# Output projection's second half and first routed expert of a hybrid encoder block: other waits, other queues, another order

## Chip, cores, metric

One core of a Trainium2 chip runs the whole block in one launch. The metric is device microseconds of that core; lower is better. Engines are named as in the profile: PE (TensorE matmul), DVE (VectorE), ACT (ScalarE), POOL (GpSimd), SP (SyncE, which here only issues DMAs).

## What is computed

One encoder layer on 512 tokens of width 1024, all float32. The part that matters here is the last third:

```python
mix = jnp.concatenate([rec, att], axis=-1) @ w_out[l]      # recurrence group | attention group
x = x + g1[:, None, :] * mix
h2 = _rms(x, norm2_g[l]) * (1.0 + sc2[:, None, :]) + sh2[:, None, :]
x = x + g2[:, None, :] * _hier_moe(h2, ...)                # top-1 group of 4, top-2 of its 4 experts
...
# _hier_moe: logits = hf @ w_rg + b_rg, hf @ w_re + b_re; then for each of the 16 experts
he = jax.nn.silu(hf @ w1[e]) * (hf @ w3[e])
y = y + combine[:, e:e + 1] * (he @ w2[e])
```

`g1, sh2, sc2, g2` are slices of `silu(c) @ w_ada + b_ada`. Before this come the adaLN norm, one input projection, a gated linear recurrence (4 heads) and a sparse attention (8 heads).

## The kernel before

Each weight piece (128 x 1024) is split into two fp32r halves, `wh` (a cast on ACT) and `wl` (the rest, a subtraction on DVE), and a product is three matmuls: high by high, low by high, high by low. The program has two parts. Up to line 1304 a planner (`Desk`) runs generators as tasks: each `yield` names an engine, marks that must be set, or a free slot, and the planner picks the next task by a planned time and a rank from `RANKS`. What comes out is a fixed order of instructions on each engine; at run time every engine takes its own list in order, and so does every queue: a DMA that waits holds what stands behind it on the issuing engine. From line 1305 on the order is that of the code.

- `ada_gen` (line 993) computes the vectors g1, sh2, sc2, g2 on DVE: 64 loads `dd` of 256 KB, issued by SP (line 1002), each followed by one DVE accumulation `acc<-dd` with 6 `dd` buffers. Eight loads make a group of 512 columns; then PE sums over partitions (`a<-acc,ones`), ACT copies, and POOL writes the group to `modD` in DRAM (line 1030). `mod_rows` (line 988, on POOL) reads a vector back, spread over all partitions. Groups 0 and 1 are g1, 2 and 3 sh2, 4 and 5 sc2, 6 and 7 g2.
- `rows_gen` (line 1110) starts when all eight groups are done: it reads `gs2b`, `sh2b`, `g2b`, multiplies the norm weights in, transposes both vectors on PE, and folds them into the router's weights `wr` and bias `cb`.
- `out_gen` (line 1148) is the output projection, `z<-wh,mix`. Half 0 takes the recurrence heads; half 1 takes the attention heads and starts when attention, `rows` and `early` (the first eight expert weights' loads) are done. Half 1 runs over 4 tiles of 128 tokens by 2 column halves, 12 matmuls each.
- `post_gen` (line 1199), per token tile: sum of squares, transpose of the residual, router logits, and a chain of small DVE operations that ends in `sel`, the two chosen experts, and `oh0`, a one-hot matrix that puts the tokens of expert 0 into slots. `store_gen` (line 1273) makes the rows `h2`: the scaling on DVE for tiles 0 and 1, on POOL and ACT for 2 and 3, and the addition of `sh2b` on POOL for all four; then ACT issues two stores. `first_gen` (line 1287) gathers expert 0's tokens on PE, `z<-oh,h`, from the finished rows.
- After line 1304: positions and weights of all experts, then `turn(0)` (the gathered tokens, split and transposed), and `up(0, ...)`, the first expert's first product, `h<-wh,xh`, 24 matmuls for `w1` and 24 for `w3`. `piece()` splits four pieces ahead, with four buffers. After the second piece of `w1`, `begin` (line 1520) runs, which makes the index lists of experts 0, 1, 2 (`match`, `place`: `oh<-slotb`, `pI<-pair,oh`) and starts the gathers of 1 and 2. All other experts gather by indirect DMA.

Of the kernel before, what the change touches and what calls it, by code (L numbers as in the profile page):

```python
# [21 lines left out]
KT = D // P  # L22
# [16 lines left out]
RANKS = "split -2 use -2 iq -1 topk 4 unit 1 att 1 hgrn 3 level 4 rows 3 ada 5 load 5 out 6 pz 7 post 0 first 3 norm -3 hx -1"  # L39
# [7 lines left out]
H2_D = 0, 1  # L47
POST_D = 1,
# [166 lines left out]
def hymba_kernel(ctx, tc, x, xT, w_ada1, w_ada, w_in, w_out, w_r, w1, w3, w2, vec, n2g, rb, rel, cst, t5, out):  # L215
# [894 lines left out]
    def rows_gen():  # L1110
        yield ["ada1"]
        mod_rows(gs2b, 4)
        mod_rows(sh2b, 2)
        mod_rows(g2b, 6)
        n2b = place4("A7", [P, D], F32, "n2b")
        sp.dma_start(n2b, bass.AP(tensor=n2g.tensor, offset=n2g.offset, ap=[[0, P], [1, D]]))
        desk.at = desk.move()
# [27 lines left out]

    h2s, routed, px = [None] * 4, {}, []

    def out_gen():
        nonlocal mw, sel, oh0, pair2
        for half in range(2):  # L1150
            if half:
                yield [("att", j) for j in range(4)] + ["rows", "early"]
# [4 lines left out]
                loads(EWB + MWB)  # L1157
# [41 lines left out]
    def post_gen(t):  # L1199
# [7 lines left out]
        for kh in range(2):  # L1207
# [8 lines left out]
            if kh:  # L1216
                mark(("turned", t))
# [14 lines left out]
        spawn(store_gen(t, h2), ("store", t), "post")  # L1232
# [21 lines left out]
        dve.tensor_scalar(oh0[:, t], slotb, p0, float(T), op0=OP.subtract, op1=OP.is_equal)  # L1254
        mark(mb)
# [49 lines left out]
    loads(LOADS1)
    OH, XE = {}, {}
# [23 lines left out]

    pn = bank([P, 4, 16])
    pe.matmul(pn, trib, sel, start=True, stop=False)
    for s in range(1, 4):
        pe.matmul(pn[:, s:], onesb, sel[:, :4 - s], start=False, stop=s == 3)
    pos = mw.tile([P, 4, 16], F32, name="pos")
    dve.scalar_tensor_tensor(pos, pn, 1.0, sel, op0=OP.add, op1=OP.mult)
    dve.tensor_scalar(posb, pos, -1.0, None, op0=OP.add)

    gate, w = (mw.tile([P, 4, n], F32, name=m) for n, m in ((2, "gate"), (1, "wn")))
    ge, comb, rest = (mw.tile([P, 4, n], F32, name=m) for n, m in ((4, "ge"), (16, "comb"), (16, "rest")))  # L1340
    dve.tensor_tensor(ge, L[:, :, 4:8], routed["g1"][:, :, 0:1].to_broadcast([P, 4, 4]), op=OP.subtract)
    dve.tensor_tensor(comb, routed["em"], routed["e2"][:, :, 0:1].to_broadcast([P, 4, 16]), op=OP.subtract)
    act.activation(ge, ge, AF.Exp)
    act.activation(comb, comb, AF.Exp)
    dve.tensor_tensor(comb, comb, sel, op=OP.mult)
    dve.reduce_sum(gate[:, :, 0:1], ge, axis=AX)
# [9 lines left out]
    pc = bank([P, 16])
    for t in range(4):
        pe.matmul(pc, onesb, sel[:, t], start=t == 0, stop=t == 3)
    cmx = mw.tile([P, 1], I32, name="cmx")
    dve.reduce_max(cmx, pc, axis=AX)  # L1360
    mixer.close()


    pq = ctx.enter_context(tc.tile_pool(name="pq", bufs=1, space=PSUM))

    def split2(n):
        if n >= NP or n in split_w:
            return
        raw = held[n]
        own = mw if n % (WPB + WX) >= WPB else wp  # L1370
        wh = own.tile([P, D], F32R, tag="wh", name="wh", bufs=WX if own is mw else WPB)
        wl = own.tile([P, D], F32R, tag="wl", name="wl", bufs=WX if own is mw else WPB)
        act.copy(wh, raw)
        dve.tensor_tensor(wl, raw, wh.bitcast(F32), op=OP.subtract)
        split_w[n] = wh, wl
        load(n + NS)

    count = [0]

    def piece():  # L1380
        n = count[0]
        count[0] += 1
        for i in range(WPB + WX):
            split2(n + i)
        return split_w.pop(n)

    pI = pq.tile([P, 16, 5], F32, tag="i", name="pI")
    XT, HS, HT = {}, {}, {}

    def place(e):  # L1390
        oh = OH.pop(e)
        for t in range(4):
            pe.matmul(pI[:, e], oh[:, t], pair2[:, t, e], start=t == 0, stop=t == 3)
        dve.tensor_scalar(idx[:, e:e + 1], pI[:, e, 0:1], pI[:, e, 1:2], float(T), op0=OP.add, op1=OP.add)
        dve.reduce_sum(wts[:, e:e + 1], pI[:, e, 2:5], axis=AX)
# [16 lines left out]
    def up(e, w, mid=None):  # L1412
# [107 lines left out]
    def begin():  # L1520
        for e in range(3):
            match(e)
            place(e)
            if e:
                gather(e)
                for n in range(*((LOADS1, LOADS2) if e == 1 else (LOADS2, NS))):
                    load(n, pool)

    turn(0)
    for e in range(16):  # L1530
        h1 = up(e, 0, None if e else begin)
# [113 lines left out]
```

## Time and profile before

| | us |
|---|---|
| median of 3 runs (lowest 763.68, highest 1159.99) | 764.67 |
| profiled execution | 764.32 |
| its span, first to last instruction | 762.5 |
| PE busy in the span | 697.0 (91%) |
| DVE busy | 637.9 (84%) |
| ACT busy | 439.8 (58%) |
| POOL busy | 126.4 (17%) |

Busy times are sums over one execution; the shares are averages over stages with different limits, so the stretches of the span are read one by one below. The profiled execution lies 1.8 us above its span and 0.35 us below the median.

### The profile page before, as it was taken

The page shows a single profiled execution, that of the slowest core. Times are in us where ns is not written, and L with a number is a line of the kernel's source. Part 1 is how long each engine was busy: PE and PEld are TensorE (multiplying, and loading weights), DVE is VectorE, ACT ScalarE, POOL GpSimd, SP SyncE. Part 2 cuts the span into 40 slices and gives each one's busy share as a digit, 9 for nine tenths or more (in the row PEclk, how much of TensorE's full clock was granted, in tenths as well). Part 3 has the DMA queues.
Part 4 walks back from the last instruction along what each step waited for, and adds up shares of the span by engine and source line. Part 5 has one row for each costly group of instructions (what it writes and reads, how often), then busy time and mean ns, then how long its engine had stood idle before and what let it go on. Part 6 is the DMA issues. An engine that isn't in the chain of part 4 may idle for free. (4 is left out here: it accounts for less than half of the span.)

```text
span 762.5 us, 10938 instructions
## 1 busy us (share of the span) xinstructions
PE 697.0 (91%) x3790; PEld 539.5 (71%) x3790; DVE 637.9 (84%) x1055; ACT 439.8 (58%) x668; POOL 126.4 (17%) x111
## 2 busy tenths in 40 slices
PE   3999999999999999998179858999999999999993
PEld 1566778877878776765068747888887888888872
DVE  4537989999999888878437577999999999999992
ACT  4326555455586465533032337777777777777870
POOL 0130010013111312210102411111111112111112
PEclk9999999999999999999569978999999999999997
DMA  9946622222221245736874779999999999999202
GB/s 362 394 143 215 221 70 84 93 73 73 80 70 48 106 142 190 272 108 197 316 283 160 266 285 377 320 362 365 364 372 362 371 358 353 359 357 365 88 11 32
DMA packets 57389, 172.85 MB, mean 227 GB/s; under 512 B 11954, under 2 KB 12530, under 8 KB 56304
## 3 DMA queue, kind: packets, MB, share of 16 engines
q1 hardware_dynamic: 45024, 150.02, 53.8%
q0 software_dynamic: 10864, 17.76, 8.3%
q10 hardware_dynamic: 1440, 4.31, 1.5%
q8 instruction: 32, 0.52, 0.3%
q14 instruction: 29, 0.24, 0.1%
HBM read 167.50 MB, written 15.24 MB: 240 GB/s over the span
## 5 line engine op out<-in xcount | busy, mean ns | idle before, releaser
L179 DVE TENSOR_TENSOR wl<-w,wh 128x1024 fp32r<-128x1024 f32 x168 | 196.7, 1217 | 6.2 <-ACT wh L179 5.6
L179 ACT CAST wh<-w 128x1024 fp32r<-128x1024 f32 x168 | 174.0, 1053 | 46.7 <-PE h L179 37.2
L179 PE MATMUL z<-hx,wh 128*128 128x512 f32 x496 | 162.7, 408 | 1.7 <-DVE hx L179 0.8
L179 PEld LDWEIGHTS z<-hx,wh 128*128 128x128 f32 x496 | 88.2, 188 | 28.2 <-issue 8.4
L179 PE MATMUL h<-wh,xh 128*128 128x512 f32 x256 | 103.3, 403 | 4.7 <-ACT wh L179 4.7
L179 ACT CAST wh<-raw 128x1024 fp32r<-128x1024 f32 x64 | 67.1, 1051 | 65.2 <-PE z L179 54.7
L179 PE MATMUL h<-wl,xh 128*128 128x512 f32 x256 | 104.2, 407 | 0.3 <-DVE wl L179 0.3
L179 PE MATMUL h<-wh,xl 128*128 128x512 f32 x256 | 102.8, 402 | 0.0
L179 PE MATMUL z<-hx,wl 128*128 128x512 f32 x248 | 97.5, 393 | 0.0
L179 DVE TENSOR_TENSOR wl<-raw,wh 128x1024 fp32r<-128x1024 f32 x64 | 82.0, 1295 | 6.6 <-ACT wh L179 6.4
L179 PEld LDWEIGHTS h<-wh,xh 128*128 128x128 f32 x256 | 49.5, 193 | 17.5 <-ACT wh L179 4.8
L179 PEld LDWEIGHTS h<-wl,xh 128*128 128x128 f32 x256 | 49.4, 193 | 12.3 <-DVE wl L179 0.8
L179 PEld LDWEIGHTS h<-wh,xl 128*128 128x128 f32 x256 | 49.2, 192 | 11.8
L1318 POOL DMA_INDIRECT out_dram<-yo,idx x16 | 36.0, 2250 | 126.5 <-DVE yo L179 126.5
L179 PE MATMUL y<-wh,hh 128*128 128x512 f32 x128 | 53.4, 417 | 2.0 <-DVE yo L179 2.0
L179 PEld LDWEIGHTS z<-hx,wl 128*128 128x128 f32 x248 | 46.6, 188 | 10.8 <-DVE wl L179 0.7
L179 PE MATMUL y<-wl,hh 128*128 128x512 f32 x128 | 51.3, 401 | 0.0
L179 PE MATMUL y<-wh,hl 128*128 128x512 f32 x128 | 51.2, 400 | 0.0
L179 PE MATMUL z<-wh,mix 128*128 128x512 f32 x128 | 48.1, 428 | 0.0
L179 DVE SCALAR_TENSOR_TENSOR acc<-dd,cT,acc 128x512 f32<-128x512 f32 x56 | 45.4, 810 | 2.5 <-DMA dd<-in_w_ada_dram 1.7
L1313 POOL DMA_INDIRECT xe<-h2D,idx x15 | 16.4, 1090 | 136.6 <-DMA out_dram<-yo,idx 63.7
L179 POOL TENSOR_TENSOR dd<-b 128x512 f32<-128x512 f32 (+1 forms) x14 | 16.5, 1197 | 93.4 <-PE a L179 79.0
(292 smaller groups left out, 1169.8 us busy)
## 6 DMA issues: line engine op xcount, KB each, us to landing
w<-in_w_dram SPq DMA_DIRECT2D x163, 512.0 KB, 11.3
raw<-in_w_in_dram SPq DMA_DIRECT2D x33, 512.0 KB, 3.3
dd<-in_w_ada_dram SPq DMA_DIRECT2D x64, 256.0 KB, 4.0
raw<-in_w_dram SPq DMA_DIRECT2D x24, 512.0 KB, 10.4
chunk<-in_w_ada_dram SPq DMA_DIRECT2D x8, 1024.0 KB, 9.0
raw<-in_w_out_dram SPq DMA_DIRECT2D x8, 512.0 KB, 3.3
lineR<-lineD POOLq DMA_DIRECT2D x4, 640.0 KB, 17.6
w<-in_w_dram POOLq DMA_DIRECT2D x5, 512.0 KB, 8.1
```

The costliest lines, as they stand in the source:

```text
L179: r = f(*a, **k)
L1313: pool.indirect_dma_start(out=dst, out_offset=None, in_=h2D, in_offset=bass.IndirectOffsetOnAxis(ap=ix, axis=0), bounds_check=T - 1, oob_i ...
L1318: pool.indirect_dma_start(out=out, out_offset=bass.IndirectOffsetOnAxis(ap=ix, axis=0), in_=y, in_offset=None, bounds_check=T - 1, oob_is_ ...
```

## The change

The ada loads go from SP's queue to POOL's. `rows_gen` reads `sh2b` and `gs2b` after group 5 instead of after group 7, and `g2b` is read by a task of its own; half 1 no longer waits for `rows`, only for the opening of the memory that the ada groups held. The scaled rows `h2 = xm * gs2b` are made on DVE for all four tiles, the factor `ss2` goes into `oh0`, and `sh2b` comes in through eight matmuls with one row; so expert 0 is gathered before the rows are finished, and these are finished on DVE afterwards. The first four expert pieces are split while half 1 runs. Copies of the transposed residual are all on ACT. After the planner's part, `turn(0)` comes first, and the weights and index lists are spread over `up(0)` and the following product.

```diff
-RANKS = "split -2 ... norm -3 hx -1"
+RANKS = "split -2 ... norm -3 hx -1 store 8 early 9"
-H2_D = 0, 1
-POST_D = 1,
...
-                sp.dma_start(t, w_ada[k * P:(k + 1) * P, 2 * D + g * 512:2 * D + g * 512 + 512])
+                pool.dma_start(t, w_ada[k * P:(k + 1) * P, 2 * D + g * 512:2 * D + g * 512 + 512])
...
-        desk.at += 2500
+            if g == 5:
+                mark("ada_rows")
...
-        yield [("hgrn", 3), "ada0"] + ["ada1"] * DD_R
+        yield [("hgrn", 3), ("split", NZ + 3), "ada0"] + ["ada1"] * DD_R
...
+        mark("early_open")
...
     def rows_gen():
-        yield ["ada1"]
-        mod_rows(gs2b, 4)
-        mod_rows(sh2b, 2)
-        mod_rows(g2b, 6)
         n2b = place4("A7", [P, D], F32, "n2b")
...
+        yield ["ada_rows"]
+        desk.at += 2500
+        mod_rows(gs2b, 4)
+        desk.at = mod_rows(sh2b, 2)
+        yield ["mw"]
...
+    def gate_gen():
+        yield ["ada1"]
+        desk.at += 2500
+        desk.at = mod_rows(g2b, 6)
...
-                yield [("att", j) for j in range(4)] + ["rows", "early"]
+                yield [("att", j) for j in range(4)] + ["early_open"]
...
-            eng, cp_ = (dve, dve.tensor_copy) if kh in POST_D else (act, act.copy)
-            yield eng.name
-            cp_(hT[:, kh * 4:kh * 4 + 4], pt)
+                spawn(scale_gen(t, h2), ("scaled", t), "store")
+            yield "act"
+            act.copy(hT[:, kh * 4:kh * 4 + 4], pt)
             mark(mb)
+            yield ["rows"]
...
+        dve.tensor_scalar(oh0[:, t], oh0[:, t], ss2[:, t:t + 1], None, op0=OP.mult)
...
+    def scale_gen(t, h2):
+        yield ["rows"]
+        yield "dve"
+        dve.tensor_tensor(h2, xm[t], gs2b, op=OP.mult)
...
+    def store(t, h2):
+        dve.scalar_tensor_tensor(h2, h2, ss2[:, t:t + 1], sh2b, op0=OP.mult, op1=OP.add)
         act.dma_start(h2D[t * P:(t + 1) * P, :], h2)
         act.dma_start(out[t * P:(t + 1) * P, :], xm[t])
...
+        for k in range(KT):
+            yield "pe"
+            pe.matmul(px[k // 4][:, k % 4], sh2b[0:1, k * P:(k + 1) * P], ones[0:1], start=False, stop=False)
         for t in range(4):
-            yield [("store", t), ("sel", t)] + [("pr", 3)] * (t > 0)
+            yield [("scaled", t), ("sel", t)]
...
+    def first_weights_gen():
+        yield ["early"]
+        for n, piece in ((0, 4), (3, 5), (1, 6), (2, 7)):
+            yield [("used", NZ + piece)]
+            yield "act"
+            split2_high(n)
+            if n != 2:
+                yield [("sel", 3)] * (n == 1)
+                yield "dve"
+                split2_low(n)
...
+    turn(0)
+    split2_low(2)
+    store(3, h2s[3])
...
         for n in range(4):
-            if n == 2 and mid:
-                mid()
             wh, wl = piece()
+            if e == 0:
+                begin(4 * w + n)
...
+    def begin(n):
+        if n == 0:
+            match(1)
+            place(1, 0, 2)
+            gather(1)
...
+        if n == 2:
+            weigh()
+        if n == 4:
+            match(2)
+            place(2)
+            gather(2)
...
+        if n == 6:
+            match(0)
+            place(0)
+            place(1, 2, 5)
```

On PE, where half 1 begins: `a<-acc,ones` and `a<-cs,vc` are the last ada group's sums, `z<-wh,mix` half 1, and `sh2b`, `gs2b`, `shT` the router vectors. Before:

```order
L179 MATMUL a<-acc,ones 32x128
L179 MATMUL a<-cs,vc 32x128
L179 MATMUL a<-cs,sh2b 128x128 x4
L179 MATMUL a<-cs,gs2b 128x128 x4
L179 MATMUL o<-wr,shT 128x20 x4
L179 MATMUL a<-cs,sh2b 128x128 x4
L179 MATMUL a<-cs,gs2b 128x128 x4
L179 MATMUL o<-wr,shT 128x20 x4
L179 MATMUL z<-wh,mix 128x512
```

And the change, at the same place:

```order
L177 MATMUL a<-acc,ones 32x128
L177 MATMUL a<-cs,vc 32x128
L177 MATMUL z<-wh,mix 128x512
L177 MATMUL z<-wl,mix 128x512
L177 MATMUL z<-wh,mix 128x512 x2
L177 MATMUL z<-wl,mix 128x512
L177 MATMUL z<-wh,mix 128x512
L177 MATMUL a<-cs,sh2b 128x128 x4
```

The vectors' transposes moved from ahead of half 1 into it; the sums of the last ada group still stand ahead of the first `z`.

On POOL, from the write of ada group 5 (the first `modD` here) on, in the change; before, POOL had three `modD` writes and three reads there and no load:

```order
L1028 DMA modD<-acc 4x128
L987 DMA gs2b<-modD 128x1024
L987 DMA sh2b<-modD 128x1024
L1000 DMA dd<-in_w_ada_dram 128x512 x8
L1028 DMA modD<-acc 4x128
L1000 DMA dd<-in_w_ada_dram 128x512 x5
L1028 DMA modD<-acc 4x128
L987 DMA g2b<-modD 128x1024
```

The last thirteen ada loads stand behind two `modD` writes and two reads of `modD` on one queue.

On DVE, from the last tile's `oh0` on. Before, the positions and weights of all experts came first (`pos` to `cmx`), then `xl` of `turn(0)` and the splits:

```order
L179 TENSOR_SCALAR sel<-er 128x16
L179 TENSOR_SCALAR oh_3629<-slotb,a 128x128
L179 SCALAR_TENSOR_TENSOR pos<-a,sel 128x64
...
L179 TENSOR_REDUCE cmx<-a 128x1
L179 TENSOR_TENSOR xl<-z,xh 128x512 x2
L179 TENSOR_TENSOR wl<-w,wh 128x1024 x5
L179 TENSOR_TENSOR oh<-slotb,posb 128x512
```

In the change, with the index list of expert 1 (`oh<-slotb,posb`), which PE needs ahead of the first `h<-wh,xh`, as the last row but one:

```order
L177 TENSOR_SCALAR oh_3574<-oh_3574,ss_3077 128x128
L177 SCALAR_TENSOR_TENSOR h_3623<-h_3623,ss_3077,sh2b 128x1024
L177 TENSOR_TENSOR wl<-w,wh 128x1024
L177 SCALAR_TENSOR_TENSOR h_3721<-h_3721,ss_3077,sh2b 128x1024
L177 SCALAR_TENSOR_TENSOR h_3793<-h_3793,ss_3077,sh2b 128x1024
L177 TENSOR_TENSOR xl<-z,xh 128x512 x2
L177 TENSOR_TENSOR wl<-w,wh 128x1024
L177 SCALAR_TENSOR_TENSOR h_3880<-h_3880,ss_3077,sh2b 128x1024
L177 SCALAR_TENSOR_TENSOR pos<-a,sel 128x64
L177 TENSOR_SCALAR posb<-pos 128x64
L177 TENSOR_TENSOR oh<-slotb,posb 128x512
L177 TENSOR_SCALAR idx<-pI 128x1
```

Four finished rows `h`, two splits and the tokens' `xl` now stand between the last choice of experts and that list.

## Rows read from the trace of the kernel before

**Rows 1.** Stretches: PE, PEld, DVE, ACT, POOL busy us (instructions), PEclk, DMA share, GB/s
```profile
355.00:390.00 35.00, 13.03 (x100) 9.68 (x100) 14.73 (x21) 7.04 (x14) 3.98 (x10) 0.61 0.79 282
390.00:430.00 40.00, 36.62 (x185) 29.54 (x184) 26.96 (x58) 12.10 (x28) 9.49 (x4) 0.91 0.56 206
430.00:445.60 15.60, 9.79 (x93) 9.44 (x93) 9.02 (x35) 6.53 (x13) 4.71 (x2) 0.98 0.82 318
445.60:464.80 19.20, 16.47 (x60) 12.14 (x61) 14.48 (x20) 8.42 (x10) 5.52 (x7) 0.75 0.93 344
500.00:600.00 100.00, 100.00 (x484) 80.96 (x483) 99.81 (x118) 78.96 (x89) 17.79 (x11) 1.00 1.01 372
```

**Rows 2.** Timeline 356 to 391: start us, us, engine, operation [idle before <-releaser]
```profile
356.97 0.57 POOL L1030 DMA_DIRECT2D modD<-acc  x1 [9.75 <-ACT acc L179]
...
363.04 0.69 DVE L179 TENSOR_TENSOR mix<-sq,mix 128x512 fp32r<-128x512 f32 x1
...
364.17 5.47 DVE L179 SCALAR_TENSOR_TENSOR acc<-dd,cT,acc 128x512 f32<-128x512 f32 x7
...
369.79 0.68 PE L179 MATMUL a<-acc,ones 128*32 128x128 f32 x8 [5.52 <-DVE acc L179]
...
371.52 0.54 POOL L1030 DMA_DIRECT2D modD<-acc  x1 [6.07 <-ACT acc L179]
...
383.06 1.09 PE L179 MATMUL a<-cs,sh2b 128*128 128x128 f32 x4 [12.16 <-DMA sh2b<-modD]
...
390.10 0.77 PE L179 MATMUL z<-wh,mix 128*128 128x512 f32 x1
```

**Rows 3.** Instructions on the tile dd: its 64 loads from issue to landing
```profile
DMA to landing us min/median/max: 2.6/4.0/5.7
```

**Rows 4.** Timeline 242 to 246, POOL
```profile
242.54 0.84 POOL L1030 DMA_DIRECT2D modD<-acc  x1 [14.13 <-DVE q L179]
245.02 0.58 POOL L989 DMA_DIRECT2D g1b<-modD  x1 [1.65 <-DMA modD<-acc]
```

**Rows 5.** Timeline 407 to 425: a POOL addition and the same DVE operation beside it and without
```profile
407.57 2.38 POOL L179 TENSOR_TENSOR h<-h,sh2b 128x1024 f32<-128x1024 f32 x1 [29.07 <-DVE h L179]
407.66 2.31 DVE L179 TENSOR_SCALAR gm<-gm 128x4 f32<-128x4 f32 x1
...
424.84 0.17 DVE L179 TENSOR_SCALAR gm<-gm 128x4 f32<-128x4 f32 x1
```

**Rows 6.** Timeline 414 to 453: from half 1's last matmul to the first expert
```profile
414.60 1.27 DVE L179 SCALAR_TENSOR_TENSOR h<-xm,ss,gs2b 128x1024 f32<-128x1024 f32 x1
429.49 0.40 PE L179 MATMUL z<-wh,mix 128*128 128x512 f32 x1
437.62 0.17 DVE L179 TENSOR_SCALAR sel<-er 128x16 bf16<-128x16 f32 x1
445.65 0.77 PE L179 MATMUL h<-wh,xh 128*128 128x512 f32 x1 [4.72 <-ACT wh L179]
452.70 0.68 DVE L179 TENSOR_TENSOR oh<-slotb,posb 128x512 bf16<-128x512 bf16 x1
```

**Rows 7.** Timeline 447 to 465, PE: matmuls of the first expert's up(0)
```profile
447.29 0.63 PE L179 MATMUL h<-wh,xl 128*128 128x512 f32 x1
...
451.13 0.63 PE L179 MATMUL h<-wh,xl 128*128 128x512 f32 x1
...
454.79 0.48 PE L179 MATMUL h<-wh,xh 128*128 128x512 f32 x1
...
458.41 0.49 PE L179 MATMUL h<-wh,xh 128*128 128x512 f32 x1
...
464.57 0.39 PE L179 MATMUL h<-wh,xl 128*128 128x512 f32 x1
```

**Rows 8.** The page's groups: the splits of expert pieces, count, busy, mean ns
```profile
L179 DVE TENSOR_TENSOR wl<-w,wh 128x1024 fp32r<-128x1024 f32 x168 | 196.7, 1217 | 6.2 <-ACT wh L179 5.6
L179 ACT CAST wh<-w 128x1024 fp32r<-128x1024 f32 x168 | 174.0, 1053 | 46.7 <-PE h L179 37.2
```

More of the change, by code (lines that the diff above doesn't have):

```diff
@@ L38 @@
 WINDOW = 100
-RANKS = "split -2 use -2 iq -1 topk 4 unit 1 att 1 hgrn 3 level 4 rows 3 ada 5 load 5 out 6 pz 7 post 0 first 3 norm -3 hx -1"
+RANKS = "split -2 use -2 iq -1 topk 4 unit 1 att 1 hgrn 3 level 4 rows 3 ada 5 load 5 out 6 pz 7 post 0 first 3 norm -3 hx -1 store 8 early 9"
 ADA_LEAD = 3
@@ L1156, in out_gen @@
                 area[0] = mw, TMP2
-                loads(EWB + MWB)
+                for n in range(EWB, EWB + MWB):
+                    load(n)
                 for n, w, v in (("g1", 8, -MARK), ("gm", 8, None), ("em", 16, None), ("e8", 8, None),
@@ L1231, in post_gen @@
         mark(mr)
-        spawn(store_gen(t, h2), ("store", t), "post")
+        spawn(store_gen(t, h2), ("store", t), "store")
         r = routed
@@ L1287, in first_gen @@
     def first_gen():
-        yield ["out", ("store", 0), ("sel", 0), ("turned", 3)] + [("add", 1, 1, t) for t in range(4)]
+        yield ["out", ("sel", 0)] + [("add", 1, 1, t) for t in range(4)]
         for _ in range(2):
@@ L1299, in first_gen, with split2, split2_high, split2_low @@
                           start=False, stop=t == 3 and k % 4 == 3)
+            mark(("px", t))
     spawn(rows_gen(), "rows", "rows")
+    spawn(gate_gen(), "gate", "rows")
     spawn(out_gen(), "out", "out")
     spawn(first_gen(), "first", "first")
+    def split2(n):
+        if n < NP and n not in split_w:
+            split2_high(n)
+            split2_low(n)
+            load(n + NS)
+    def split2_high(n):
+        own = mw if n % (WPB + WX) >= WPB else wp
+        wh = own.tile([P, D], F32R, tag="wh", name="wh", bufs=WX if own is mw else WPB)
+        wl = own.tile([P, D], F32R, tag="wl", name="wl", bufs=WX if own is mw else WPB)
+        act.copy(wh, held[n])
+        split_w[n] = wh, wl
+    def split2_low(n):
+        wh, wl = split_w[n]
+        dve.tensor_tensor(wl, held[n], wh.bitcast(F32), op=OP.subtract)
+    def first_weights_gen():
[3 more added lines that the diff above has]
+            yield "act"
+            split2_high(n)
+            if n != 2:
+                yield [("sel", 3)] * (n == 1)
+                yield "dve"
+                split2_low(n)
+    spawn(first_weights_gen(), "first_weights", "early")
     run()
     loads(LOADS1)
+    for n in range(WPB + WX):
+        load(n + NS)
     OH, XE = {}, {}
@@ L1328, in match @@
                            posb[:, :, e:e + 1].to_broadcast([P, 4, P]), op=OP.is_equal)
[L1331 to L1346, printed above, removed]
@@ L1356, in hymba_kernel @@
[L1356 to L1395, printed above, removed]
+    XT = {}
@@ L1410, in turn @@
         XT[e] = xh, xl
-    def up(e, w, mid=None):
+    turn(0)
+    split2_low(2)
+    store(3, h2s[3])
+    pn = bank([P, 4, 16])
+    pe.matmul(pn, trib, sel, start=True, stop=False)
+    for s in range(1, 4):
+        pe.matmul(pn[:, s:], onesb, sel[:, :4 - s], start=False, stop=s == 3)
+    pos = mw.tile([P, 4, 16], F32, name="pos")
+    dve.scalar_tensor_tensor(pos, pn, 1.0, sel, op0=OP.add, op1=OP.mult)
+    dve.tensor_scalar(posb, pos, -1.0, None, op0=OP.add)
+    gate, w = (mw.tile([P, 4, n], F32, name=m) for n, m in ((2, "gate"), (1, "wn")))
@@ new lines, in hymba_kernel, with weigh @@
+    ge, comb, rest = (mw.tile([P, 4, n], F32, name=m) for n, m in ((4, "ge"), (16, "comb"), (16, "rest")))
+    cmx = mw.tile([P, 1], I32, name="cmx")
+    def weigh():
+        dve.tensor_tensor(ge, L[:, :, 4:8], routed["g1"][:, :, 0:1].to_broadcast([P, 4, 4]), op=OP.subtract)
+        dve.tensor_tensor(comb, routed["em"], routed["e2"][:, :, 0:1].to_broadcast([P, 4, 16]), op=OP.subtract)
+        act.activation(ge, ge, AF.Exp)
+        act.activation(comb, comb, AF.Exp)
+        dve.tensor_tensor(comb, comb, sel, op=OP.mult)
+        dve.reduce_sum(gate[:, :, 0:1], ge, axis=AX)
+        dve.reduce_sum(gate[:, :, 1:2], comb, axis=AX)
+        dve.tensor_tensor(w, gate[:, :, 0:1], gate[:, :, 1:2], op=OP.mult)
+        dve.reciprocal(w, w)
+        dve.tensor_tensor(comb, comb, w.to_broadcast([P, 4, 16]), op=OP.mult)
+        dve.tensor_copy(pair2[:, :, :, 2], comb)
+        dve.tensor_tensor(rest, comb, pair2[:, :, :, 2], op=OP.subtract)
+        dve.tensor_copy(pair2[:, :, :, 3], rest)
+        dve.tensor_tensor(pair2[:, :, :, 4], rest, pair2[:, :, :, 3], op=OP.subtract)
+        dve.tensor_scalar(pos, pos, -1.0, None, op0=OP.add)
@@ new lines, in hymba_kernel, with piece, place @@
+    mixer.close()
+    pq = ctx.enter_context(tc.tile_pool(name="pq", bufs=1, space=PSUM, reuse_waits="tile"))
+    count = [0]
+    def piece():
+        n = count[0]
+        count[0] += 1
+        for i in range(WPB + WX):
+            split2(n + i)
+        return split_w.pop(n)
+    pI = pq.tile([P, 16, 5], F32, tag="i", name="pI")
+    HS, HT = {}, {}
+    def place(e, a=0, b=5):
+        oh = OH[e]
+        for t in range(4):
+            pe.matmul(pI[:, e, a:b], oh[:, t], pair2[:, t, e, a:b], start=t == 0, stop=t == 3)
+        if a == 0:
+            dve.tensor_scalar(idx[:, e:e + 1], pI[:, e, 0:1], pI[:, e, 1:2], float(T), op0=OP.add, op1=OP.add)
+        if b == 5:
+            dve.reduce_sum(wts[:, e:e + 1], pI[:, e, 2:5], axis=AX)
@@ L1413, in up, with largest @@
+    def largest():
+        pc = pq.tile([P, 16], F32, tag="c", name="pc")
+        for t in range(4):
+            pe.matmul(pc, onesb, sel[:, t], start=t == 0, stop=t == 3)
+        dve.reduce_max(cmx, pc, axis=AX)
+    def up(e, w):
         xh, xl = XT[e]
@@ L1518, in further @@
                 add_rows(y, ix)
[L1520 to L1529, printed above, removed]
+    def begin(n):
[3 more added lines that the diff above has]
+            gather(1)
+            for m in range(LOADS1, LOADS2):
+                load(m, pool)
+        if n == 2:
[4 more added lines that the diff above has]
+            gather(2)
+            for m in range(LOADS2, NS):
+                load(m, pool)
+        if n == 6:
+            match(0)
+            place(0)
+            place(1, 2, 5)
     for e in range(16):
-        h1 = up(e, 0, None if e else begin)
+        h1 = up(e, 0)
         if 0 < e < 14:
@@ L1541, in hymba_kernel @@
             gather(e + 2)
+        if e == 14:
+            largest()
         if e:
```

23 lines of the change are left out of this document (3 added, 20 removed).

## Prediction

> **What bounds the kernel now.** I read the busy shares first, then the span in stretches, then the timeline of the one stretch where PE is not full. From 500 to 600 us PE is busy for 100 of 100 us and DVE for 99.8 [rows 1]: the expert stage runs at PE's pace, so whatever moves the end of the first expert's first product (464.8 us) moves the end of the kernel by as much. The 40 us before 355 are full as well, and the change leaves PE's list there word for word. What can be won lies from 355 to 465. From 355 to 390 PE is busy for 13.0 of 35 us at a mean granted clock of 0.61 [rows 1]. The attention's last `mix` is ready on DVE at 363.73, but half 1 begins only at 390.10; PE sits for 12.16 us until the read of `sh2b` has landed and then spends 7.0 us, from 383.06 to 390.10, on the router vectors [rows 2]. From 390 to 430 it is full again (36.6 of 40), from 430 to 445.6 half idle (9.8 of 15.6), and the first expert from 445.6 to 464.8 has 16.5 of 19.2, at a granted clock of 0.75 [rows 1].
>
> **The change, part by part.** I follow one path: start of half 1, its end, the last choice of experts (`sel` of tile 3), the first `h<-wh,xh`, the end of `up(0)`.
>
> *Start of half 1.* The router vectors leave the path, but PE's list still has the sums of the last ada group ahead of the first `z`. So the start is now set by the ada groups 6 and 7, and these change too. Group 5's `modD` is written at 356.97 as before [rows 2]. Behind it on POOL now stands the read of `gs2b`, which waits until that write has landed: from the start of such a write to the read that follows it took 2.48 us [rows 4], so it issues at 359.5, the read of `sh2b` at 360.1, and the next `dd` loads from 360.6 on, 0.55 us apart. A load took 2.6 to 5.7 us to land, 4.0 in the median [rows 3]; behind the two reads of 512 KB I take 365.1 for the first. DVE's list puts five accumulations behind `mix` (363.73); at 5.47 / 7 = 0.78 us each [rows 2] group 6 ends at 365.1 + 3.9 = 369.0. Group 7 has three loads landed by then; its other five stand behind group 6's `modD`. From the end of group 7 at 369.64 to that write were 1.9 us [rows 2], so I take the write for 370.9, the next load for 371.4, its landing for 375, and five more accumulations for 378.9. PE's sums took 1.3 us from there (369.79 to the copy) at the lower clock; half 1 starts at 380.3 instead of 390.10: -9.8. Bounds: with no load late it would be 363.73 + 3.9 + 6.0 + 1.3 = 374.9 (-15.2); with landings of 5.7 us at both places 383.7 (-6.4).
>
> *Half 1.* 40.0 us before, 36.6 of them busy [rows 1]. Added are the vectors' transposes and small products, 7.0 us at the lower clock before [rows 2] and about half of that at the upper: I take 5. Gone are DVE stalls: a POOL addition of 2.38 us held a DVE operation of 0.17 us for 2.31 [rows 5]; there were six such POOL operations, all removed, and PE's idle time of 3.4 us in this stretch is the most that can come back; I take 2.5. The split of the first expert pieces adds two `wl` of 1.22 us [rows 8] to DVE, which had 13 of 40 us free [rows 1]: nothing. Sum +2.5; bounds -1 and +6.
>
> *Last matmul of half 1 to the last `sel`.* Before 429.89 to 437.79, 7.9 us [rows 6]. Here the chain is the same but for one stall behind a POOL addition, like that of [rows 5] but shorter; I put it at 1.1 us: 6.8; bounds -2 and +1.5.
>
> *Last `sel` to the first `h`.* Before 437.79 to 445.65, 7.9 us [rows 6]. Now PE's first `h` stands behind the index list of expert 1, and DVE's list has ahead of that list: `oh0` twice (0.6), four rows `h` at 1.27 [rows 6] = 5.1, two `wl` at 1.22 [rows 8] = 2.4, `xl` (1.3), `pos` and `posb` (0.4), and the list itself, 0.68 [rows 6]. That is 10.5 us of DVE. Two handovers must be added: `xl` waits for ACT, which first has to issue the store of the third row and then casts `xh` (I put 1.5 us for it), and PE answers DVE at both ends (0.7 each, my estimate). That is 13.4 us: +5.5. What was to hide the finishing of the rows (PE's work on expert 0) stands behind it in the list. Bounds: +3 if the ACT handover costs nothing, +9 if PE's 32 gather matmuls run at half the clock.
>
> *`up(0)`.* Before 19.15 us: matmuls at 0.427 us apart from 447.29 to 451.13 and up to 458.41, then at 0.237 apart (458.41 to 464.57), and a pause from 451.56 to 454.79 for `begin` [rows 7]. The splits of the first four pieces are ready beforehand now, but they did not hold it up before by more than 1 us. In place of one pause there are two: `begin` at the fifth and at the seventh piece puts an index list on DVE behind the split of a piece whose buffer PE frees only with the matmul just before. Each costs a cast 1.05 and a subtraction 1.22 [rows 8], the list 0.68 [rows 6], and 0.5 for the handovers: 3.5 us, twice. `weigh` at the third piece is hidden by three pieces that are split ahead. With the clock rising as late as before (12.8 us after the first `h`): 24 matmuls at 0.427 = 10.3, pause 3.5, then 24 at 0.237 = 5.7 and again 3.5, in all 23.0 to 23.3: +4.2. Bounds: -1 and +8.5 (all 48 at the lower clock, 20.5 + 7).
>
> *Before 355.* The 64 ada loads now issue from POOL, 0.54 to 0.84 us each [rows 2, 4], 35 to 54 us in a POOL that is busy 126 of 762 us; in POOL's list the masks of the attention stand behind loads that wait for a free `dd`. PE's list is the same and has no slack. I take 0, because the loads wait for DVE operations that come before the masks' use in DVE's own list; bounds -1 and +17 (64 x (0.84 - 0.58), if every load's longer issue came through).
>
> One rule of the Trainium skill speaks against this move: SBUF — State Buffer, section "SBUF: two separate sides", says that a DMA issued from GpSimd has its descriptors written by GpSimd, and that it cannot write them while a VectorE operation in a two-port mode holds the shared port; that page of the skill has an example that grows from about 620 to about 3100 ns. By that, an estimate from the page SBUF — State Buffer, 64 loads could cost POOL up to 64 x 2.5 = 160 us more. By that rule the fourth case below would hold; the trace agrees only weakly: the issues beside a busy DVE took 0.84 and 0.58 us, the one beside an idle DVE 0.54 [rows 2, 4].
>
> *Sum.* -9.8 + 2.5 - 1.1 + 5.5 + 4.2 + 0 = +1.3. From the profiled 764.3 us (span 762.5 and 1.8 around it): 765.6. The median shown, 764.67, is 0.35 us above that execution, so both stand for the same. A measurement of this kernel can tell about 2% from no change: below 749 or above 780.
>
> **The rivals.**
> 1. *The queue does not bite.* The last thirteen loads land in time (half 1 at 374.9, -15.2), the handovers of the rows are short (+4.0), and the clock is up for the first expert (48 x 0.237 + 7.0 = 18.4, -0.8). Sum -15.2 + 2.5 - 1.1 + 4.0 - 0.8 = -10.6: 753.7. For it: DVE's accumulations ran at 0.78 us apart in the tail, so SP's loads were never late. Against it: nothing on POOL could hold those. Only with half 1 as short as its busy time as well (a further 4 us) does this fall below 749.
> 2. *The lower clock stays.* The gather of expert 0 and all of `up(0)` run at the lower of the two levels, 1.2 instead of 2.4 GHz: +8.5 instead of +4.2 for `up(0)` and +3 for the gather's 32 matmuls: 773. For it: PE idles longer ahead of the first `h`, and the granted clock was 0.75 there already. Against: it was 0.98 from 430 to 445.6 [rows 1].
> 3. *The change does not do what it says:* half 1 stays behind the ada groups. That is in the sum already, as 380.3; were the tail as late as the bound (383.7), the time would be 769.
> 4. *Slower: POOL's queue holds the attention.* A mask behind a load that waits reaches DVE late, and with it PE, in the stretches that have no slack. Price: +17 from the bound above, 765.6 + 17 = 782.6. It decides from the point where a mask is ready later than DVE gets to it; the DVE list leaves a few us for that, and POOL is free for most of the time, which speaks against it.
>
> **How the numbers follow.** Forecast 0.55 (with the third case), its own range 758 to 772; first rival 0.17, second 0.16, fourth 0.12. The range 750 to 781 takes in the first two rivals and the near half of the fourth. Faster by over 2%: the far part of the first rival, with half 1 shorter too, 0.10. Slower by over 2%: the fourth, 0.12. Within 2%: 0.78.
>
> **What would show it.** In the profile after: first `z<-wh,mix` of half 1 near 380, behind an `a<-acc,ones` that waited for DVE's `acc`, and DVE's `acc` idle for some 4 us in group 7 with `dd` as releaser; POOL's `gs2b` read about 2.5 us behind a `modD`. No DVE `gm` or `e` operation over 1 us from 390 to 430. Some 13 us from the last `sel` to the first `h<-wh,xh`, with DVE busy all along. Two pauses of 3 to 4 us in `up(0)`, at `pI<-pair,oh`. It would be wrong if half 1 started by 375, if the first `h` followed the last `sel` by less than 10 us, or if DVE or PE idled before 355 behind a POOL mask.

## The result and the profile after

The changed kernel takes 775.5 us (median of 5 runs, 774.09 to 779.13), the kernel before 764.5 beside it. The ratio of the mean times, without one execution of the kernel before that took 1159.99 us, is 1.0153, 95% interval 1.012 to 1.0186. That is slower by 11 us, where +1 was forecast. The time lies in the stated range of 750 to 781 us, but above the forecast's own 758 to 772, and the miss is large enough to have a cause of its own. The profiled execution took 779.13 us (span 777.1), the slowest of the five and 3.6 us above their median.

The stretches of the changed kernel, with the columns of [rows 1]:

```profile
355.00:390.00 35.00, 14.48 (x105) 10.01 (x100) 18.90 (x25) 7.49 (x14) 12.01 (x23) 0.66 0.70 246
390.00:430.00 40.00, 39.23 (x233) 34.00 (x232) 22.84 (x73) 15.49 (x35) 0.00 (x0) 0.91 0.57 213
430.00:445.60 15.60, 8.73 (x66) 8.04 (x65) 9.71 (x12) 2.12 (x3) 0.00 (x0) 0.82 0.86 326
445.60:464.80 19.20, 10.35 (x39) 7.66 (x38) 11.29 (x25) 6.46 (x8) 5.82 (x7) 0.77 0.98 371
500.00:600.00 100.00, 95.12 (x463) 77.10 (x462) 94.14 (x108) 74.05 (x84) 33.85 (x10) 0.98 0.98 354
600.00:700.00 100.00, 96.84 (x471) 78.47 (x470) 96.58 (x115) 77.04 (x87) 43.44 (x11) 1.00 0.99 363
```

From 390 to 430 PE is fuller than before (39.2 of 40). From 430 to 465 PE does 7 us less work. New is the last part: the expert stage, where PE had 100 of 100 us [rows 1], has 95 and 97. The path of the prediction, from the timelines of the changed kernel:

```profile
364.67 0.75 DVE L177 SCALAR_TENSOR_TENSOR acc<-dd,cT,acc 128x512 f32<-128x512 f32 x1 [1.74 <-DMA dd<-in_w_ada_dram]
375.04 1.54 DVE L177 SCALAR_TENSOR_TENSOR acc<-dd,cT,acc 128x512 f32<-128x512 f32 x2 [3.79 <-DMA dd<-in_w_ada_dram]
379.82 0.68 PE L177 MATMUL a<-acc,ones 128*32 128x128 f32 x8 [9.30 <-DVE acc L177]
380.86 0.80 PE L177 MATMUL z<-wh,mix 128*128 128x512 f32 x1
...
419.43 0.39 PE L177 MATMUL z<-wh,mix 128*128 128x512 f32 x1
425.95 0.17 DVE L177 TENSOR_SCALAR sel<-er 128x16 bf16<-128x16 f32 x1
429.00 0.29 DVE L177 TENSOR_SCALAR oh<-slotb,a 128x128 f32<-128x128 bf16 x1 [2.87 <-PE a L177]
437.81 1.29 DVE L177 TENSOR_TENSOR xl<-z,xh 128x512 fp32r<-128x512 f32 x2 [2.67 <-ACT xh L177]
442.56 0.27 PE L177 MATMUL pI<-pair,oh 128*128 128x2 bf16 x4 [6.87 <-DVE oh L177]
442.69 0.77 PE L177 MATMUL h<-wh,xh 128*128 128x512 f32 x1
455.85 0.27 PE L177 MATMUL pI<-pair,oh 128*128 128x5 bf16 x4 [5.44 <-DVE oh L177]
464.17 0.27 PE L177 MATMUL pI<-pair,oh 128*128 128x5 bf16 x4 [3.05 <-DVE oh L177]
465.50 0.63 PE L177 MATMUL h<-wl,xh 128*128 128x512 f32 x1
465.93 0.63 PE L177 MATMUL h<-wh,xl 128*128 128x512 f32 x1
470.23 0.60 ACT L177 ACTIVATE s<-h 128x512 f32<-128x512 f32 x1
```

In rows like the first, "[1.74 <-DMA dd...]" is idle time of the engine and what ended it. ACT's `s<-h` follows the end of `up(0)` at once; in the kernel before it stands at

```profile
465.97 0.60 ACT L179 ACTIVATE s<-h 128x512 f32<-128x512 f32 x1
```

so the changed kernel is 4.3 us late there. (By the start of `up(0)`'s last matmul, 469.77 against the 464.57 of [rows 7], it is 5.2 us late; `s<-h` wins 0.9 back.) Its span is 14.6 us longer: the other 10.3 us are lost in the expert stage, on the same instructions.

What is lost there shows on POOL. In the kernel before every expert's gather (`xe`) and scatter (`out_dram`) look like this, the scatters 18.25 us apart:

```profile
527.70 2.30 POOL L1318 DMA_INDIRECT out_dram<-yo,idx  x1 [6.93 <-DVE yo L179]
537.98 1.04 POOL L1313 DMA_INDIRECT xe<-h2D,idx  x1 [7.98 <-DMA out_dram<-yo,idx]
545.96 2.31 POOL L1318 DMA_INDIRECT out_dram<-yo,idx  x1 [6.94 <-DVE yo L179]
```

In the changed kernel, POOL first, then DVE and PE:

```profile
512.06 10.87 POOL L1366 DMA_INDIRECT out_dram<-yo,idx  x1 [6.79 <-DMA xe<-h2D,idx]
...
543.53 1.04 POOL L1361 DMA_INDIRECT xe<-h2D,idx  x1 [7.97 <-DVE s L177]
551.39 10.86 POOL L1366 DMA_INDIRECT out_dram<-yo,idx  x1 [6.82 <-DMA xe<-h2D,idx]
562.55 1.04 POOL L1361 DMA_INDIRECT xe<-h2D,idx  x1 [0.30 <-issue]
...
531.57 1.41 DVE L177 SCALAR_TENSOR_TENSOR yo<-y,wts,g2b 128x512 f32<-128x512 f32 x2 [2.98 <-DMA out_dram<-yo,idx]
...
534.16 0.50 PE L177 MATMUL h<-wl,xh 128*128 128x512 f32 x1 [2.76 <-DVE wl L177]
```

Five of the sixteen scatters take 10.9 us on POOL instead of 2.3. Such a scatter lands up to 19.4 us after its issue, against 11.1 at most before; its source `yo` has one buffer, so DVE's next `yo` stands 1.7 to 3.0 us for it (here the scatter of 512.06 holds up the `yo` of 531.57); behind it in DVE's list is the `wl` of a weight piece, and PE stands for that. Nothing in the text of the change touches these instructions.

### The profile page after: what moved, and what is told of

The parts are those of the page before. It is cut to its first block, busy times and chain, and to the rows that moved or that the text cites. A ratio compares the mean times of both kernels' runs of the same rounds, so it can differ in the third digit from the quotient of the medians.

```text
span 777.1 us, 10963 instructions
## 1 busy us (share of the span) xinstructions
PE 697.5 (90%) x3810; PEld 543.3 (70%) x3810; DVE 636.9 (82%) x1061; ACT 438.8 (56%) x670; POOL 190.1 (24%) x169
## 4 chain that ended last, share of the span: by engine, by line
PE 52%; DMA 21%; DVE 12%; issue 9%; ACT 2%; POOL 1%; SPq 0%; ACTq 0%; POOLq 0%; DVEq 0%
PE z L177 26%; PE a L177 13%; DMA out_dram<-yo,idx 12%; PE h L177 7%; DVE wl L177 6%; DMA dd<-in_w_ada_dram 2%; PE u L177 2%; PE o L177 2%; DMA raw<-in_w_dram 2%; DMA xe<-h2D,idx 2%; PE y L177 1%; DMA chunk<-in_w_ada_dram 1%; ACT wh L177 1%; DVE yo L177 1%; DVE acc L177 1%
## 5 line engine op out<-in xcount | busy, mean ns | idle before, releaser
L177 DVE TENSOR_TENSOR wl<-w,wh 128x1024 fp32r<-128x1024 f32 x168 | 197.2, 1217 | 15.7 <-ACT wh L177 14.7
L177 PE MATMUL h<-wl,xh 128*128 128x512 f32 x256 | 104.7, 409 | 10.3 <-DVE wl L177 10.3
L1366 POOL DMA_INDIRECT out_dram<-yo,idx x16 | 78.9, 4934 | 131.4 <-DVE yo L177 112.4
L177 PEld LDWEIGHTS z<-hx,wl 128*128 128x128 f32 x248 | 46.8, 189 | 10.3
L1361 POOL DMA_INDIRECT xe<-h2D,idx x15 | 16.6, 1108 | 150.0 <-DMA out_dram<-xm 57.5
L1000 POOL DMA_DIRECT2D dd<-in_w_ada_dram x64 | 34.7, 545 | 50.9 <-DVE acc L177 29.5
```

Source lines behind the costliest of these rows:

```text
L177: r = f(*a, **k)
L1000: pool.dma_start(t, w_ada[k * P:(k + 1) * P, 2 * D + g * 512:2 * D + g * 512 + 512])
L1361: pool.indirect_dma_start(out=dst, out_offset=None, in_=h2D, in_offset=bass.IndirectOffsetOnAxis(ap=ix, axis=0), bounds_check=T - 1, oob_i ...
L1366: pool.indirect_dma_start(out=out, out_offset=bass.IndirectOffsetOnAxis(ap=ix, axis=0), in_=y, in_offset=None, bounds_check=T - 1, oob_is_ ...
```

## The experiments

Times of one group of experiments share runs of the kernel before (764.3 to 765.0 us in the median), and the ratio is that of the mean times.

**x1 and x2: is it the dd loads on POOL's queue?** My first theory (Q): the 64 more loads leave POOL's queue in a state in which the scatters stall. x1 is the changed kernel with one line back, x2 the kernel before with the same line changed:

```diff
-                pool.dma_start(t, w_ada[...])
+                sp.dma_start(t, w_ada[...])
```

> The changed kernel with the 64 dd loads back on SP's queue, everything else of the change kept. Theory Q (the dd loads on POOL's queue leave that queue in a state in which every second scatter of an expert's rows is held about 8.5 us longer, the one yo buffer comes free late, DVE stands, and PE stands about 2 us for each): the scatters' mean goes from 4934 ns back to about 2250 ns, none takes 10.9 us, PE is busy 99 us or more of 500 to 600 and of 600 to 700, and the time is 764 to 768 us, 8 to 10 below the changed kernel. Theory W (the expert stage starves because the half 1 and routing work left the weight loads late): PE stays at 95 to 97 of 500 to 700 and the time stays at 773 to 778 us.

> The kernel before with one line changed: the 64 dd loads on POOL's queue. Theory Q: four to six of the 16 scatters take about 10.9 us instead of 2.3, PE is no longer busy all of 500 to 700 (about 96 of each 100), and the time is 770 to 776 us. Theory W: the scatters keep 2.3 us, and the time is 762 to 767 us.

x1: 771.75 us, ratio 1.0087 (1.0059 to 1.0116). x2: 770.81 us, 1.0082 (1.0055 to 1.011). Both went against Q. x1 keeps four scatters of 10.9 us and PE at 96.1 and 95.9 of 100; x2 has none, with PE at 100 and 100. So theory Q fell, although the time of x2 lies in the range that Q gave for it: no scatter is held there. W, that late weight loads starve the experts, has PE's share in x1 right but not its time, and x2 is 4 us above its range. The line has a price of its own: in x2 half 1 begins at 396.34 us instead of 390.10 [rows 2], and these 6.2 us arrive at the end whole. In x1 it begins at 374.82 instead of 380.86.

**x3 and x4: the way to the end of up(0).** x3 puts each step of `begin` ahead of the weight splits of its piece:

```diff
-            wh, wl = piece()
             if e == 0:
                 begin(4 * w + n)
+            wh, wl = piece()
```

> The changed kernel with each step of begin(n) issued ahead of the weight splits of its piece, not behind them. Theory U (the two pauses in up(0), 5.4 and 3.1 us, are the one-hot that stands in DVE's queue behind the wl of a piece whose buffer PE frees only as it stops): both pauses fall under 1.5 us, up(0) ends 5 to 8 us earlier, and the time falls as much, to 768 to 771 us. Rival (the expert stage is bound by its weights or by POOL's queue, and swallows a gain at its start): the pauses go, but the time falls by under 2 us.

x4 computes the positions and the index list of expert 1 ahead of `turn(0)` (and drops `match(1)` from `begin(0)`):

```diff
-    turn(0)
-    split2_low(2)
-    store(3, h2s[3])
...
     dve.tensor_scalar(posb, pos, -1.0, None, op0=OP.add)
+    match(1)
+    turn(0)
+    split2_low(2)
+    store(3, h2s[3])
```

> The changed kernel with the positions (pn, pos, posb) and match(1) issued ahead of turn(0), the low part of piece 2 and the last row's store. Theory S (the first expert's matmuls wait for the one-hot of expert 1, whose chain stands behind xl, wl and the last h on DVE): the wait of 6.9 us ahead of the first pI becomes about 3, the first h starts 2.5 to 3.5 us earlier after the last sel (16.6 us in the changed kernel), and the time falls by 2 to 3 us, to about 772.5. Rival: the first h is then held by ACT's xh, which stands behind the rows' DMA issues, and the time falls by under 1 us.

x3: 767.85 us, 1.0048 (1.0023 to 1.0072); the pauses fall from 5.44 and 3.05 to 2.64 and 1.70 us, not under 1.5, and `s<-h` comes at 461.33, 8.9 us earlier, 5.5 of them behind the first `h`. x4: 770.91 us, 1.0086 (1.0061 to 1.011). Its wait ahead of the first `pI` is 1.27 us and the first `h` follows the last `sel` by 10.1 us (16.6 in the changed kernel), more than expected, but a pause of 5.44 us in `up(0)` becomes 7.82, where part of what was won waits. In both, gains at the start reach the end, so the stage does not swallow them; both keep the held scatters (five of 10.9 us and one of 9.1).

**x5 and x6: the layout.** Q's fall left the question what the changed kernel has and x1 to x4 kept, but x2 lacks. Two things differ in the rows of the expert stage. In every kernel with held scatters, PE's matmuls of `h` follow each other faster: in the changed kernel

```profile
495.10 0.39 PE L177 MATMUL h<-wh,xh 128*128 128x512 f32 x1
495.32 0.39 PE L177 MATMUL h<-wl,xh 128*128 128x512 f32 x1
495.55 0.39 PE L177 MATMUL h<-wh,xl 128*128 128x512 f32 x1
```

they come 0.2267 us apart (mean of 39 from 485 to 500 us), before 0.2334 (47), at a granted clock of 1.00 in both. And DVE has no pause. By a pause I mean that an operation starts later than straight behind the one before it; here it is read from the starts of `hl` and of the next `wl`. In the kernel before they are 0.71 us apart, with 0.03 us idle between them; in the changed kernel, ahead of a held scatter, they are 0.60 apart, and the two overlap. ACT's cast `wh` of the same piece (the first of the two in its row, 1.05 us long) is shown below each:

```profile
504.78 0.68 DVE L179 TENSOR_TENSOR hl<-pt,hh 128x512 fp32r<-128x512 f32 x1
505.49 2.36 DVE L179 TENSOR_TENSOR wl<-w,wh 128x1024 fp32r<-128x1024 f32 x2
...
504.41 2.00 ACT L179 CAST wh<-w 128x1024 fp32r<-128x1024 f32 x2
```

```profile
546.84 0.68 DVE L177 TENSOR_TENSOR hl<-pt,hh 128x512 fp32r<-128x512 f32 x1
547.44 2.35 DVE L177 TENSOR_TENSOR wl<-w,wh 128x1024 fp32r<-128x1024 f32 x2
...
545.80 2.00 ACT L177 CAST wh<-w 128x1024 fp32r<-128x1024 f32 x2
```

So the pause is a wait for ACT: before, the cast ends at 505.46 and `wl` starts 0.03 us later; in the changed kernel it ended at 546.85, 0.6 us ahead. In all twelve traces, from 480 to 720 us, `wl` follows that cast by 0.03 us wherever the starts are 0.66 us or more apart, and by 0.13 to 0.58 where they are 0.60. That the faster matmuls free ACT and let it run ahead of DVE fits this; no run changes their pace without the layout.

In the built programs `xh` and `xl`, which these matmuls load, begin at byte 179008 and 183104 of each partition before, a multiple of 64, and at 182176 and 186272 in the changed kernel, 32 bytes off one: `turn(0)`, moved ahead, now allocates them before some small tiles. x5 adds to the changed kernel, x6 to the kernel before, one tile that nothing uses:

```diff
+    mw.tile([P, 8], F32, name="pad")
     def turn(e):
         xh = mw.tile([P, KT, P], F32R, tag="xh", name="xh", bufs=1)
```

> The changed kernel with one unused tile of 32 bytes ahead of xh and xl, which puts these two tiles at a multiple of 64 bytes, as they are in the kernel before; nothing else differs. Theory A (the layout of the changed kernel put xh and xl 32 bytes off a multiple of 64, PE's matmuls of h became faster, 0.227 us apart instead of 0.233, DVE then has no pause left between an expert's gather and its scatter, and POOL's scatter is held to 10.9 us): the h matmuls come 0.233 us apart again, no scatter takes 10.9 us, the scatters come 18.25 us apart, PE is busy 99 us or more of 500 to 600 and of 600 to 700, and the time falls by 7 to 10 us, to about 766.5. Rival Q2 (the held scatters come from the order or the time of the earlier DMAs of POOL's queue): they stay, and the time stays at 773 to 778 us.

> The kernel before with the same unused tile of 32 bytes ahead of xh and xl, which puts them 32 bytes off a multiple of 64, as in the changed kernel. Theory A: the h matmuls come 0.227 us apart, four to six scatters take 10.9 us, PE is busy about 96 of each 100 us from 500 to 700, and the time rises by 6 to 10 us, to about 772. Rival Q2: the scatters keep 2.3 us, and the time stays within 2 us of 764.3 or falls by up to 2.

x5: 766.07 us, 1.0022 (1.0001 to 1.0042). x6: 774.71 us, 1.0127 (1.0104 to 1.0151). 32 unused bytes are worth 9.4 us one way (775.5 to 766.07) and 9.9 the other (764.86 to 774.71). Instructions on the tile `yo` by POOL (first line: sixteen scatters, ns min/median/max) and the stretch from 500 to 600 us, x5:

```profile
L1366 POOL DMA_INDIRECT out_dram<-yo,idx x16: 1544/2309/2362, 491.5 to 753.8; - x16
500.00:600.00 100.00, 100.00 (x489) 81.13 (x486) 99.84 (x117) 78.84 (x90) 17.77 (x11) 1.00 1.01 370
```

and x6:

```profile
L1318 POOL DMA_INDIRECT out_dram<-yo,idx x16: 1542/2307/10867, 492.1 to 765.5; - x16
500.00:600.00 100.00, 96.14 (x474) 77.91 (x473) 95.68 (x114) 75.89 (x87) 43.43 (x11) 1.00 1.00 364
```

From 600 to 700 us PE is busy for 100.00 in x5 and 96.24 in x6. The matmuls of `h` are 0.2332 us apart in x5 and 0.2291 in x6 (0.227 was expected there). The list tile `oh` moved as well, but x4, where it lies 32 bytes off, and the changed kernel, where it does not, both have held scatters. `hl` lies 32 bytes off in x5 as in the changed kernel, and at a multiple of 64 before. Over the built programs of both kernels and x1 to x6, `xh` and `xl` are the only tiles of SBUF whose offset from a multiple of 64 bytes goes with the held scatters. W falls here too: the loads of x5 are those of the changed kernel, in the same order.

**x7: is it the layout, or the pause?** The layout and the fast matmuls stay, and DVE gets its pause by a second copy of `hh` on ACT, which stands ahead of the cast `wh`:

```diff
         act.copy(a, pt)
+        act.copy(a, pt)
         dve.tensor_tensor(b, pt, a.bitcast(F32), op=OP.subtract)
```

> The changed kernel with each copy of hh on ACT made twice (0.59 us more of ACT for an expert, the value is the same), so that DVE's hl comes later and DVE pauses between the gather and the scatter; layout and order as in the changed kernel. Theory L (a pause of DVE of a few tenths between gather and scatter is what lets the scatter through in 2.3 us): the h matmuls keep 0.227 us, but no scatter takes 10.9 us, PE is busy 98 us or more of 500 to 600 and of 600 to 700, and the time falls by 6 to 9 us, to 766 to 769. Rival (it is PE's pace or the layout itself that holds the scatter): the held scatters stay and the time stays at 774 to 779.

x7: 767.73 us, 1.0048 (1.0031 to 1.0065), with more work than the changed kernel and 7.8 us less time. The `h` matmuls come 0.22 to 0.23 us apart, with short waits for DVE once or twice an expert (the mean is 0.233, so part of the expectation failed: the pause is paid for by PE). DVE's list shows the pause, `hl` 0.67 ahead of `wl`, and no scatter is held. It is `wl` that starts later, 0.03 us behind ACT's cast, and not `hl` as was expected:

```profile
542.81 0.68 DVE L177 TENSOR_TENSOR hl<-pt,hh 128x512 fp32r<-128x512 f32 x1
543.48 2.36 DVE L177 TENSOR_TENSOR wl<-w,wh 128x1024 fp32r<-128x1024 f32 x2
...
539.51 1.04 POOL L1361 DMA_INDIRECT xe<-h2D,idx  x1 [7.97 <-PE y L177]
547.44 2.30 POOL L1366 DMA_INDIRECT out_dram<-yo,idx  x1 [6.90 <-DVE yo L177]
```

The pause need not show as idle time: `hl` ends at 543.49, after `wl` has started, and DVE is busy for 100.00 us from 500 to 600, more than the 94.14 of the changed kernel. So with the layout of the changed kernel a later `wl` frees the scatters (x7), and without its layout `wl` is as late (x5): the layout acts through the pause.

**x8, x9, x10: the parts together.** x8 is the changed kernel with the edits of x3, x4 and x5; x9 is x8, x10 is x5, each with the line of x1.

> The changed kernel with the positions and match(1) ahead of turn(0), begin(n) ahead of the weight splits of its piece, and the 32-byte tile: the two orders that shorten the way to the end of up(0) and the layout of the kernel before. If the gains add (up(0) ends 8 to 10 us earlier, the expert stage keeps 18.25 us for an expert), the time is 754 to 758 us, below the kernel before. If the expert stage swallows an earlier start, it is 762 to 766 us.

> As x8 (both orders and the 32-byte tile), with the 64 dd loads back on SP's queue. In x1 that edit took 3.75 us off the changed kernel while its scatters were still held. If POOL's queue costs half 1 its start by itself, the time is 750 to 754 us, 3 to 6 below x8, and the first matmul of half 1 comes before 376 us (380.9 in the changed kernel). If what it gains is taken back before the end of up(0) (the rows' work and the weight pieces are then what is late), it is within 2 us of x8's 756.1.

> As x5 (the changed kernel with the 32-byte tile), with the 64 dd loads back on SP's queue: the price of POOL's queue where no scatter is held. If the queue costs what x2 showed on the kernel before (6.5 us), the time is 759 to 761 us. If x1's 3.75 us is the price, it is 762 to 763. If nothing is left of it, 765 to 767.

x8: 756.13 us, 0.9897 (0.9879 to 0.9915). x9: 752.69 us, 0.983 (0.9795 to 0.9865). x10: 760.83 us, 0.9945 (0.9926 to 0.9964). The gains add. Without held scatters the queue costs 5.2 us (x10 against x5) and 3.4 with the better orders (x9 against x8); x10 lies in the range that x2's price gave. x9 is 12 us below the kernel before, on these rows of its path and of its expert stage:

```profile
373.97 0.79 PE L177 MATMUL z<-wh,mix 128*128 128x512 f32 x1
...
455.99 0.60 ACT L177 ACTIVATE s<-h 128x512 f32<-128x512 f32 x1
500.00:600.00 100.00, 100.00 (x487) 80.93 (x486) 99.91 (x117) 78.77 (x89) 17.51 (x12) 1.00 1.00 361
```

## Why the prediction was right, and where it was wrong

The time fell into the stated range of 750 to 781 us, but that is luck: it lies above the forecast's own 758 to 772, near the 773 of the second rival, and most of the 11 us have a cause that no rival named. The terms, each against the profiled execution after:

| step | forecast | seen | change forecast | change seen |
|---|---|---|---|---|
| start of half 1 | 380.3 | 380.86 | -9.8 | -9.2 |
| half 1 | 42.5 | 39.0 | +2.5 | -0.8 |
| last matmul to last `sel` | 6.8 | 6.3 | -1.1 | -1.6 |
| last `sel` to first `h` | 13.4 | 16.6 | +5.5 | +8.7 |
| first `h` to the end of `up(0)` | 23.3 | 27.5 (to `s<-h`; 20.3 before) | +4.2 | +7.2 (+8.2 to its last matmul) |
| after that | 0 | span +14.6 less the above | 0 | +10.3 |

- **Start of half 1** came as worked out, by the same two waits of DVE for `dd` (3.79 us in group 7; "some 4" was said). The bound "with no load late", 374.9, is what x1 shows with the loads on SP: 374.82. So the loads' move to POOL's queue gives back 6 us of what the new order of PE's work wins.
- **Half 1** was mis-sized. I added 5 us for the vectors and took only 2.5 back. Within half 1 PE's idle time fell from 3.3 us of 39.8 to 1.3 of 39.0, and its busy time rose by only 1.2, at a granted clock of 0.94 (0.91 before): 5 us was too much for them. The POOL stalls are gone as said: no `gm` or `e` operation of DVE from 390 to 430 takes over 0.2 us, where one took 2.31 [rows 5].
- **Last `sel` to first `h`**: the list was right, and it stood on DVE as counted, but two handovers were too short, and no row stood behind either figure: `oh` waited 2.87 us for PE, whose list has part of the gather of expert 0 ahead (0.7 was put), and `xl` waited 2.67 us for ACT (1.5 was put). It stays within the bound of +9. The same order in x1, x5, x7 and x10 took 14.7 to 15.4, so some of it varies. x4 shows that the chain is an order, not a need: 10.1 us.
- **up(0)** has its two pauses, at `pI` behind DVE's `oh`, 5.44 and 3.05 us, 8.5 where 7.0 was put. What I missed is PE's clock: I let it rise once and stay. After each pause the matmuls come 0.43 us apart again (465.50 to 465.93), the lower of the two levels: some 32 of the 48 do, where I had put 24. That is part of rival 2, which had up to +8.5 for it.
- **Before 355** was right: nothing was lost (the mask of POOL's queue, rival 4, did not come), and the last `mix` ends at 362.93 us (363.73 before); the 64 issues took 0.545 us each in the mean, 0.60 at most. The Trainium skill's rule weighed there (SBUF — State Buffer, section "SBUF: two separate sides") was not seen in these plain loads.
- **The step that failed** is the first claim of the argument: "the expert stage runs at PE's pace, so whatever moves the end of the first expert's first product (464.8 us) moves the end of the kernel by as much". The first half was read off PE's 100 of 100 us. But the same row has DVE at 99.8 [rows 1], and the stage stood on a start: 0.71 us from `hl` to `wl` between an expert's gather and its scatter, where 0.60 is straight behind. The busy share does not tell this, for x7 has DVE at 100.00 and no held scatter. With the new layout PE's `h` matmuls came 3% faster, DVE lost that pause, five scatters were held 8.5 us, and the scatters came 19.25 us apart in the mean instead of 18.25 (from 493.93 to 705.68 in eleven steps), some 10 us in all. No term of the sum had a place for it: I read the change as order and queues, and not that a moved allocation shifts tiles by 32 bytes.

With the layout put back the sum holds: x5 is 1.2 us above the kernel before, +1.3 was forecast. That the two agree so closely is luck as well: in x5 half 1 came 3.8 us below its term, and the way from the last `sel` to the last matmul of `up(0)` 5.5 us above.

## What to carry to other kernels

Where two engines are full at once, ask which small pause of the second one something else lives on, and read it from the starts of its operations, not from its busy share; "PE is at 100%" does not say that a faster PE makes the stage faster. When a step is moved that allocates tiles, compare the addresses of all tiles behind it, and repeat the measurement with the old layout before the order is judged. Put an index list ahead of the weight splits it does not need: x3 and x4 are two such orders, and with the layout they turn a loss of 11 us into a gain of 9.

## What the runs showed of the hardware

- **32 bytes of offset went with another pace of the `h` matmuls.** With the loaded tiles `xh` and `xl` at a multiple of 64 bytes these 128x512 matmuls follow 0.2334 us apart, 32 bytes off it 0.2267 (0.2291 in x6), at a granted clock of 1.00. It is no rule for every matmul: those of `y` load `hh`, which lies 32 bytes off in both kernels and in x1 to x7, and they come some 0.233 us apart in all of these. Only two offsets were tried, and the reason was not looked for.
- **A POOL scatter goes through in 2.3 us or is held to 10.9, and a start of DVE that is later by hundredths of a us decides.** The twelve traces hold 156 scatters that follow a gather within 11 us. 26 took 9.1 to 10.9 us: ahead of each, `hl` began at most 0.61 us before the next `wl`, and DVE did not stand from the gather on. 130 took 2.1 to 2.4: ahead of each, `hl` began at least 0.66 us before `wl`, or DVE stood for 1.7 us or more. The held ones begin 7.82 to 7.86 us after the gather (two at 6.97), but so do two that went through (7.85 in x9, 7.87 in x10, after a pause): it is not the time. The five of the changed kernel last until DVE's list reaches operations that read PSUM: they end 1.5 us after `idx<-pI` starts and 0.75 us after `xl` starts:

```profile
551.03 4.62 DVE L177 TENSOR_TENSOR wl<-w,wh 128x1024 fp32r<-128x1024 f32 x4
555.57 0.68 DVE L177 TENSOR_TENSOR oh<-slotb,posb 128x512 bf16<-128x512 bf16 x1
556.17 4.62 DVE L177 TENSOR_TENSOR wl<-w,wh 128x1024 fp32r<-128x1024 f32 x4
560.71 0.21 DVE L177 TENSOR_SCALAR idx<-pI 128x1 int32<-128x1 f32 x1
560.85 0.15 DVE L177 TENSOR_REDUCE wts<-pI 128x1 f32<-128x3 f32 x1
560.91 0.68 DVE L177 TENSOR_TENSOR s<-s,h 128x512 f32<-128x512 f32 x1
561.51 1.28 DVE L177 TENSOR_TENSOR xl<-pt,xh 128x512 fp32r<-128x512 f32 x2
```

  (551.39 + 10.86 = 562.25; all of DVE's list from 551.1 to 560.7 reads SBUF alone.) Which of these operations lets the scatter go is not shown: the two of 9.1 us, in x3 and x4, end 0.4 us after `s<-s,h` starts and 0.2 us ahead of `xl`. That DVE holds something which POOL needs is the reading that fits, and no run shows what it is. The Trainium skill (SBUF — State Buffer, section "Who interferes with whom") says that DVE operations in a two-port mode contend with GpSimd, and whichever starts first shuts the other out; a `tensor_tensor`, it says, has no such mode, but one with both inputs in SBUF contends with GpSimd's reads. Here it is `tensor_tensor` operations with both inputs in SBUF that fill the time. That rule alone does not settle it, for scatters that went through in 2.3 us ran beside the same `wl` operations (x7, 547.44). Why a pause ahead of the scatter decides, and not one beside it, stays open.
